# Four window pairs per q and k load, with four rows per partition, in a local attention kernel

## The chip, the cores and the metric

One core of one Trainium2 chip runs the kernel. The metric is device time in microseconds (us), lower is better. Each version was timed beside runs of the kernel before on the same chip. The experiments ran on four chips, on which the kernel before took 977.5 to 978.3 us (medians).

## The reference

Attention inside windows of 64 rows; B=4, S=4096, D=1536, all float32.

```python
q_w = q.reshape(B, nw, W, D)            # W = 64; k_w, v_w likewise
logits = np.einsum('bnwd,bnud->bnwu', q_w, k_w) * D ** -0.5
attn = softmax(logits)                  # over u (cut)
out = np.einsum('bnwu,bnud->bnwd', attn, v_w)
```

The inputs are 302.0 MB and the output 100.7 MB. The arithmetic per byte is small.

## The kernel before

PE is the matmul engine, ACT and DVE the scalar and the vector engine; POOL and SP issue transfers (DMAs). The inputs lie in HBM, tiles in SBUF, and PE writes to PSUM. The kernel works on one pair of windows (128 rows) at a time, 128 pairs in all. q, k and v are cast to bf16 by the DMA itself, issued from POOL. PE transposes q and k in 128x128 blocks, ACT or DVE copies the transposes out of PSUM, PE forms the scores, ACT the exponentials, PE the product with v, and ACT or DVE scales it. SP issues the stores.

```python
q_pool = ctx.enter_context(tc.tile_pool(name="q_pool", bufs=3))   # k_pool, v_pool: 3 too
# ... t_pool, s_pool, o_pool: 2 buffers; PSUM pools: 2, 2 and 3
for it in range(n_pairs):
    r0 = it * P
    nc.gpsimd.dma_start(out=q_nat, in_=qf[r0 : r0 + P, :])   # [128, 1536]; k and v likewise
    for src, dst in ((q_nat, qT), (k_nat, kT)):
        for g in range(DCH // TGRP):                         # 2 groups of 6 blocks
            ptile = ptr_pool.tile([P, TGRP, P], bf16, name="ptile")
            for j in range(TGRP):
                nc.tensor.transpose(ptile[:, j, :], src[:, c * P : (c + 1) * P], ident)
            nc.any.tensor_copy(out=dst[:, g * TGRP : (g + 1) * TGRP, :], in_=ptile)
    # ... scores st (12 matmuls), est = exp(st), row sums, recip
    # ... po = est x v by 64x64 blocks, o_sb = po * recip
    nc.sync.dma_start(out=of[r0 : r0 + P, :], in_=o_sb)
```

The softmax here doesn't subtract the row's maximum and nothing guards it: scores larger than these inputs give would overflow.

## Time and profile before

| | |
|---|---|
| Time, median | 977.8 us (13 runs, 977.3 to 978.8) |
| HBM traffic over the span | 412 GB/s |
| DMA, slices at 9 tenths or more | 39 of 40 |
| PE, ACT, DVE busy | 60%, 42%, 28% |

From the page of the kernel before: the span, busy times, the DMA slices (one digit for each fortieth of the span, in tenths), and the traffic.

```profile
span 976.4 us, 14179 instructions
...
PE 586.0 (60%) x5632; PEld 405.1 (41%) x5632; DVE 273.2 (28%) x513; ACT 412.6 (42%) x641; POOL 203.4 (21%) x390
...
DMA  9999999999999999999999999999999999999996
...
q0 software_dynamic: 55296, 151.02, 78.8%
q1 hardware_dynamic: 18432, 100.67, 26.1%
q8 instruction: 44, 0.72, 0.3%
...
HBM read 301.99 MB, written 100.66 MB: 412 GB/s over the span
```

No compute engine is near full, and DMA has no hole but at the end. The queue lines give packets, MB and the share of 16 engines' time. q0 is the loads (bf16 as landed, half of what is read), q1 the stores. Together they show 105%, as the times of packets overlap. In the DMA records of the trace, a load piece is one partition's row: 6 KB read, 3 KB landed, taking 248 ns of one engine. 49152 of the q0 packets are such pieces and 6144 are 4-byte completion writes, 16 to each of the 384 load DMAs (one per DMA engine).

The page's groups of the kernel before, transposes copied out of PSUM (count, then busy us and mean ns of one):

```profile
L79 ACT COPY qT<-ptile 128x768 bf16<-128x768 bf16 x254 | 202.7, 798 | 250.8 <-PE ptile L76 246.9
...
L79 DVE COPY kT<-ptile 128x768 bf16<-128x768 bf16 x128 | 70.7, 552 | 25.2 <-PE ptile L76 25.1
```

The waits of the kernel before (total us, times, longest):

```profile
PE ptile L76 <- DMA q_nat<-in_q_dram: 220.2, 65, 6.5
...
PE ptile L76 <- DMA k_nat<-in_k_dram: 101.9, 63, 2.6
```

PE waits for data for a third of the time. That is what a DMA-bound kernel looks like from PE.

### The profile page before, as it was taken

To read this page: it belongs to the slowest core of one execution; us is meant where nothing else is said; L and a number is where in the kernel's file an instruction comes from. 1 tells how busy PE (TensorE), PEld (TensorE's weight loads), DVE (VectorE), ACT (ScalarE), POOL (GpSimd) and SP (SyncE) were. 2 spreads that over 40 slices of the span, in tenths; PEclk is the share of its full clock that TensorE was granted. 3 is DMA by queue.
4 is the path that set the end of the run, shared out by engine and by line. 5 is a ranking of instruction groups with operands and counts; after the bars stand their busy time and mean duration, and the time that the engine had idled before them with its cause. 6 is when DMAs were issued, how large, how long until landed. Compare 5 with 4: busy or idle time off the path is not lost.

```text
span 976.4 us, 14179 instructions
## 1 busy us (share of the span) xinstructions
PE 586.0 (60%) x5632; PEld 405.1 (41%) x5632; DVE 273.2 (28%) x513; ACT 412.6 (42%) x641; POOL 203.4 (21%) x390
## 2 busy tenths in 40 slices
PE   5556566565565665656656556556565565565654
PEld 3344344343343443434434344344343443444433
DVE  2223232232232322322323223232232232322322
ACT  3344344443443444434434344344443443444443
POOL 3122121221221212212212222121221221212210
PEclk9676776776767767677777676776776777767676
DMA  9999999999999999999999999999999999999996
GB/s 194 255 268 253 270 261 257 275 254 264 267 253 271 261 256 269 256 267 263 255 274 259 259 270 254 268 263 255 274 259 259 270 251 271 263 255 274 252 265 184
DMA packets 73795, 252.60 MB, mean 259 GB/s; under 512 B 8192, under 2 KB 8192, under 8 KB 73728
## 3 DMA queue, kind: packets, MB, share of 16 engines
q0 software_dynamic: 55296, 151.02, 78.8%
q1 hardware_dynamic: 18432, 100.67, 26.1%
q8 instruction: 44, 0.72, 0.3%
q14 instruction: 23, 0.19, 0.0%
HBM read 301.99 MB, written 100.66 MB: 412 GB/s over the span
## 4 chain that ended last, share of the span: by engine, by line
DMA 82%; PE 9%; issue 7%; ACT 1%; POOL 1%; POOLq 0%; ACTq 0%
DMA k_nat<-in_k_dram 48%; DMA v_nat<-in_v_dram 30%; DMA q_nat<-in_q_dram 4%; PE ptile L76 4%; PE po L108 3%; PE ps L87 1%; POOL k_nat L66 1%; ACT kT L79 0%; PE ps L100 0%; ACT qT L79 0%; ACT o_sb L122 0%; POOL q_nat L65 0%; POOL v_nat L67 0%; ACT est L96 0%; POOLq L66 0%
## 5 line engine op out<-in xcount | busy, mean ns | idle before, releaser
L76 PE MATMUL ptile<-ident,q_nat 128*128 128x128 bf16 x1536 | 181.2, 264 | 220.2 <-DMA q_nat<-in_q_dram 220.2
L79 ACT COPY qT<-ptile 128x768 bf16<-128x768 bf16 x254 | 202.7, 798 | 250.8 <-PE ptile L76 246.9
L76 PE MATMUL ptile<-ident,k_nat 128*128 128x128 bf16 x1536 | 168.4, 264 | 140.5 <-DMA k_nat<-in_k_dram 101.9
L76 PEld LDWEIGHTS <-q_nat 128*128 128x128 bf16 x1536 | 128.4, 121 | 258.4 <-DMA q_nat<-in_q_dram 231.5
L76 PEld LDWEIGHTS <-k_nat 128*128 128x128 bf16 x1536 | 119.9, 118 | 214.6 <-DMA k_nat<-in_k_dram 119.5
L103 DVE RECIPROCAL recip<-ps 128x1 f32<-128x1 f32 x128 | 21.5, 168 | 635.6 <-PE ps L101 618.0
L122 DVE TENSOR_SCALAR o_sb<-po,recip 128x512 f32<-128x512 f32 x254 | 184.9, 748 | 29.9 <-PE po L115 18.4
L87 PE MATMUL ps<-qT,kT 128*128 128x128 bf16 x1536 | 170.6, 267 | 20.8 <-ACT kT L79 19.8
L122 ACT ACTIVATE o_sb<-po,recip 128x512 f32<-128x512 f32 x130 | 89.4, 688 | 147.6 <-PE po L115 146.7
L67 POOL DMA_DIRECT2D v_nat<-in_v_dram x128 | 67.6, 528 | 391.6 <-PE po L115 347.9
L108 PE MATMUL po<-v_nat,est 64*64 64x512 bf16 x384 | 148.5, 509 | 0.0
L115 PE MATMUL po<-v_nat,est 64*64 64x512 bf16 x384 | 148.4, 509 | 0.0
L87 PEld LDWEIGHTS <-kT 128*128 128x128 bf16 x1536 | 128.3, 123 | 40.3 <-ACT kT L79 36.8
L79 ACT COPY kT<-ptile 128x768 bf16<-128x768 bf16 x128 | 102.3, 799 | 56.6 <-PE ptile L76 56.6
L65 POOL DMA_DIRECT2D q_nat<-in_q_dram x128 | 68.3, 533 | 231.3 <-PE ptile L76 206.1
L66 POOL DMA_DIRECT2D k_nat<-in_k_dram x128 | 67.7, 529 | 125.2 <-DMA v_nat<-in_v_dram 84.3
L96 ACT ACTIVATE est<-ps 128x128 bf16<-128x128 f32 x128 | 35.8, 280 | 103.4 <-PE ps L87 103.4
L79 DVE COPY kT<-ptile 128x768 bf16<-128x768 bf16 x128 | 70.7, 552 | 25.2 <-PE ptile L76 25.1
L108 PEld LDWEIGHTS <-est 64*64 64x64 bf16 x384 | 41.1, 138 | 24.4 <-issue 18.8
L115 PEld LDWEIGHTS <-est 64*64 64x64 bf16 x384 | 40.8, 137 | 0.0
L100 PE MATMUL ps<-ones,est 64*64 64x1 bf16 x128 | 25.8, 201 | 3.6 <-ACT est L96 0.4
L100 PEld LDWEIGHTS <-est 64*64 64x64 bf16 x128 | 14.9, 116 | 27.3 <-ACT est L96 13.7
(11 smaller groups left out, 43.7 us busy)
## 6 DMA issues: line engine op xcount, KB each, us to landing
out_dram<-o_sb SPq DMA_DIRECT2D x128, 768.0 KB, 7.8
q_nat<-in_q_dram POOLq DMA_DIRECT2D x128, 384.0 KB, 19.1
k_nat<-in_k_dram POOLq DMA_DIRECT2D x128, 384.0 KB, 19.1
v_nat<-in_v_dram POOLq DMA_DIRECT2D x128, 384.0 KB, 16.6
```

What stands on the lines that cost most here:

```text
L65: nc.gpsimd.dma_start(out=q_nat, in_=qf[r0 : r0 + P, :])
L66: nc.gpsimd.dma_start(out=k_nat, in_=kf[r0 : r0 + P, :])
L67: nc.gpsimd.dma_start(out=v_nat, in_=vf[r0 : r0 + P, :])
L76: nc.tensor.transpose(ptile[:, j, :], src[:, c * P : (c + 1) * P], ident)
L79: nc.any.tensor_copy(out=dst[:, g * TGRP : (g + 1) * TGRP, :], in_=ptile)
L87: nc.tensor.matmul(st, kT[:, c, :], qT[:, c, :], start=(c == 0), stop=(c == DCH - 1),)
L96: nc.scalar.activation(out=est, in_=st, func=mybir.ActivationFunctionType.Exp, scale=scale)
L100: nc.tensor.matmul(rs[0:W, :], est[0:W, 0:W], ones[0:W, :], start=True, stop=True)
L103: nc.vector.reciprocal(out=recip, in_=rs)
L108: nc.tensor.matmul(po[0:W, :], est[0:W, 0:W], v_nat[0:W, c * NCOL : (c + 1) * NCOL], start=True, stop=True,)
L115: nc.tensor.matmul(po[W:P, :], est[W:P, W:P], v_nat[W:P, c * NCOL : (c + 1) * NCOL], start=True, stop=True,)
L122: nc.any.tensor_scalar(out=o_sb[:, c * NCOL : (c + 1) * NCOL], in0=po, scalar1=recip, scalar2=None, op0=mybir.AluOpType.mult,)
```

## The change

The intent: fewer and larger q/k transfers. One load brings four pairs of q, with rows 4p to 4p+3 in partition p, so that the 24 KB of a partition lie together in HBM. The row order is undone when the transposes are copied out of PSUM. v and the output stay as they were, pair by pair. Buffer counts change too, the row sums get a PSUM tile of their own (one buffer), and the first loads are issued ahead of the identity's construction.

```diff
+    RPP = 4 if n_pairs % 4 == 0 else 1
-    q_pool, k_pool, v_pool: bufs=3; s_pool, o_pool: bufs=2          (abridged)
+    qk_pool: bufs=2 (q and k tiles of four pairs), v_pool: bufs=6, s_pool: 3, o_pool: 4
+    def load_qk(it):
+        r0 = it * PAIRS_PER_IT * P
+        qt = qk_pool.tile([P, RPP, D], bf16, name="qt")
+        qsrc = qf[r0 : r0 + RPP * P, :].rearrange("(p r) d -> p r d", p=P, r=RPP)
+        nc.gpsimd.dma_start(out=qt, in_=qsrc)                        # k likewise
 ...
-                for j in range(TGRP):
-                    c = g * TGRP + j
-                    nc.tensor.transpose(ptile[:, j, :], src[:, c * P : (c + 1) * P], ident)
-                nc.any.tensor_copy(out=dst[:, g * TGRP : (g + 1) * TGRP, :], in_=ptile)
+                for j in range(RPP):
+                    nc.tensor.transpose(ptile[:, j, :], src[:, j, c * P : (c + 1) * P], ident)
+                dslice = dst[:, c, :].rearrange("d (p j) -> d p j", j=RPP, p=P)
+                nc.any.tensor_copy(out=dslice, in_=ptile.rearrange("d j p -> d p j"))
+        for m in range(PAIRS_PER_IT):
+            v_nat = prev[m] if it == 0 else load_v(pair)
             (scores, exp, sums, product with v, store: as before, for pair m)
```

More of the change, by code (lines that the diff above doesn't have):

```diff
@@ L31 @@
     assert D % P == 0 and (B * S) % P == 0
+    RPP = 4 if n_pairs % 4 == 0 else 1
+    PAIRS_PER_IT = RPP
+    n_iters = n_pairs // PAIRS_PER_IT
     qf = q.flatten_outer_dims()
@@ L38 @@
     consts = ctx.enter_context(tc.tile_pool(name="consts", bufs=1))
-    ident = consts.tile([P, P], bf16)
-    make_identity(nc, ident)
-    ones = consts.tile([P, 1], bf16)
-    nc.vector.memset(ones, 1.0)
-    q_pool = ctx.enter_context(tc.tile_pool(name="q_pool", bufs=3))
-    k_pool = ctx.enter_context(tc.tile_pool(name="k_pool", bufs=3))
-    v_pool = ctx.enter_context(tc.tile_pool(name="v_pool", bufs=3))
+    qk_pool = ctx.enter_context(tc.tile_pool(name="qk_pool", bufs=2))
+    v_pool = ctx.enter_context(tc.tile_pool(name="v_pool", bufs=6))
     t_pool = ctx.enter_context(tc.tile_pool(name="t_pool", bufs=2))
-    s_pool = ctx.enter_context(tc.tile_pool(name="s_pool", bufs=2))
-    o_pool = ctx.enter_context(tc.tile_pool(name="o_pool", bufs=2))
+    s_pool = ctx.enter_context(tc.tile_pool(name="s_pool", bufs=3))
+    o_pool = ctx.enter_context(tc.tile_pool(name="o_pool", bufs=4))
     ptr_pool = ctx.enter_context(tc.tile_pool(name="ptr_pool", bufs=2, space=bass.MemoryType.PSUM))
     ps_pool = ctx.enter_context(tc.tile_pool(name="ps_pool", bufs=2, space=bass.MemoryType.PSUM))
+    rs_pool = ctx.enter_context(tc.tile_pool(name="rs_pool", bufs=1, space=bass.MemoryType.PSUM))
     po_pool = ctx.enter_context(tc.tile_pool(name="po_pool", bufs=3, space=bass.MemoryType.PSUM))
@@ L56 @@
     assert D % NCOL == 0
-    TGRP = 6 if DCH % 6 == 0 else (4 if DCH % 4 == 0 else (2 if DCH % 2 == 0 else 1))
-    for it in range(n_pairs):
-        r0 = it * P
-        q_nat = q_pool.tile([P, D], bf16, name="q_nat")
-        k_nat = k_pool.tile([P, D], bf16, name="k_nat")
-        v_nat = v_pool.tile([P, D], bf16, name="v_nat")
-        nc.gpsimd.dma_start(out=q_nat, in_=qf[r0 : r0 + P, :])
-        nc.gpsimd.dma_start(out=k_nat, in_=kf[r0 : r0 + P, :])
-        nc.gpsimd.dma_start(out=v_nat, in_=vf[r0 : r0 + P, :])
-        qT = t_pool.tile([P, DCH, P], bf16, name="qT")
-        kT = t_pool.tile([P, DCH, P], bf16, name="kT")
+    def load_qk(it):
+        r0 = it * PAIRS_PER_IT * P
+        qt = qk_pool.tile([P, RPP, D], bf16, name="qt")
+        kt = qk_pool.tile([P, RPP, D], bf16, name="kt")
+        qsrc = qf[r0 : r0 + RPP * P, :].rearrange("(p r) d -> p r d", p=P, r=RPP)
+        ksrc = kf[r0 : r0 + RPP * P, :].rearrange("(p r) d -> p r d", p=P, r=RPP)
+        nc.gpsimd.dma_start(out=qt, in_=qsrc)
+        nc.gpsimd.dma_start(out=kt, in_=ksrc)
+        return qt, kt
@@ new lines, in load_v @@
+    def load_v(pair):
+        r0 = pair * P
+        vt = v_pool.tile([P, D], bf16, name="vt")
+        nc.gpsimd.dma_start(out=vt, in_=vf[r0 : r0 + P, :])
+        return vt
+    preq = load_qk(0)
+    prev = [load_v(p) for p in range(PAIRS_PER_IT)]
+    ident = consts.tile([P, P], bf16)
+    nc.vector.memset(ident, 0.0)
+    make_identity(nc, ident, nomemset=True)
+    ones = consts.tile([P, 1], bf16)
+    nc.vector.memset(ones, 1.0)
+    for it in range(n_iters):
+        q_nat, k_nat = preq if it == 0 else load_qk(it)
+        qT = t_pool.tile([P, DCH, RPP * P], bf16, name="qT")
+        kT = t_pool.tile([P, DCH, RPP * P], bf16, name="kT")
@@ L71 @@
         for src, dst in ((q_nat, qT), (k_nat, kT)):
-            for g in range(DCH // TGRP):
-                ptile = ptr_pool.tile([P, TGRP, P], bf16, name="ptile")
-                for j in range(TGRP):
-                    c = g * TGRP + j
+            for c in range(DCH):
+                ptile = ptr_pool.tile([P, RPP, P], bf16, name="ptile")
+                for j in range(RPP):
                     nc.tensor.transpose(
-                        ptile[:, j, :], src[:, c * P : (c + 1) * P], ident
+                        ptile[:, j, :], src[:, j, c * P : (c + 1) * P], ident
@@ L78 @@
                     )
-                nc.any.tensor_copy(
-                    out=dst[:, g * TGRP : (g + 1) * TGRP, :], in_=ptile
-                )
-        ps = ps_pool.tile([P, P + 8], fp32, name="ps")
-        st = ps[:, 0:P]
-        rs = ps[:, P : P + 1]
-        for c in range(DCH):
-            nc.tensor.matmul(
-                st,
-                kT[:, c, :],
-                qT[:, c, :],
-                start=(c == 0),
-                stop=(c == DCH - 1),
-            )
-        est = s_pool.tile([P, P], bf16, name="est")
@@ L96 @@
-        nc.scalar.activation(
-            out=est, in_=st, func=mybir.ActivationFunctionType.Exp, scale=scale
-        )
-        nc.tensor.matmul(rs[0:W, :], est[0:W, 0:W], ones[0:W, :], start=True, stop=True)
-        nc.tensor.matmul(rs[W:P, :], est[W:P, W:P], ones[W:P, :], start=True, stop=True)
-        recip = s_pool.tile([P, 1], fp32, name="recip")
-        nc.vector.reciprocal(out=recip, in_=rs)
-        o_sb = o_pool.tile([P, D], fp32, name="o_sb")
-        for c in range(D // NCOL):
-            po = po_pool.tile([P, NCOL], fp32, name="po")
-            nc.tensor.matmul(
-                po[0:W, :],
-                est[0:W, 0:W],
-                v_nat[0:W, c * NCOL : (c + 1) * NCOL],
-                start=True,
-                stop=True,
+                if RPP > 1:
+                    dslice = dst[:, c, :].rearrange("d (p j) -> d p j", j=RPP, p=P)
+                else:
+                    dslice = dst[:, c, :].unsqueeze(1)
@@ new lines @@
+                nc.any.tensor_copy(out=dslice, in_=ptile.rearrange("d j p -> d p j"))
+        for m in range(PAIRS_PER_IT):
+            pair = it * PAIRS_PER_IT + m
+            r0 = pair * P
+            v_nat = prev[m] if it == 0 else load_v(pair)
+            st = ps_pool.tile([P, P], fp32, name="st")
+            rs = rs_pool.tile([P, 1], fp32, name="rs")
+            for c in range(DCH):
+                nc.tensor.matmul(
+                    st,
+                    kT[:, c, m * P : (m + 1) * P],
+                    qT[:, c, m * P : (m + 1) * P],
+                    start=(c == 0),
+                    stop=(c == DCH - 1),
+                )
+            est = s_pool.tile([P, P], bf16, name="est")
+            nc.scalar.activation(
+                out=est, in_=st, func=mybir.ActivationFunctionType.Exp, scale=scale
@@ L114 @@
             )
             nc.tensor.matmul(
-                po[W:P, :],
-                est[W:P, W:P],
-                v_nat[W:P, c * NCOL : (c + 1) * NCOL],
-                start=True,
-                stop=True,
-            )
-            nc.any.tensor_scalar(
-                out=o_sb[:, c * NCOL : (c + 1) * NCOL],
-                in0=po,
-                scalar1=recip,
-                scalar2=None,
-                op0=mybir.AluOpType.mult,
-            )
-        nc.sync.dma_start(out=of[r0 : r0 + P, :], in_=o_sb)
+                rs[0:W, :], est[0:W, 0:W], ones[0:W, :], start=True, stop=True
+            )
@@ new lines @@
+            nc.tensor.matmul(
+                rs[W:P, :], est[W:P, W:P], ones[W:P, :], start=True, stop=True
+            )
+            recip = s_pool.tile([P, 1], fp32, name="recip")
+            nc.vector.reciprocal(out=recip, in_=rs)
+            o_sb = o_pool.tile([P, D], fp32, name="o_sb")
+            for c in range(D // NCOL):
+                po = po_pool.tile([P, NCOL], fp32, name="po")
+                nc.tensor.matmul(
+                    po[0:W, :],
+                    est[0:W, 0:W],
+                    v_nat[0:W, c * NCOL : (c + 1) * NCOL],
+                    start=True,
+                    stop=True,
+                )
+                nc.tensor.matmul(
+                    po[W:P, :],
+                    est[W:P, W:P],
+                    v_nat[W:P, c * NCOL : (c + 1) * NCOL],
+                    start=True,
+                    stop=True,
+                )
+                nc.any.tensor_scalar(
+                    out=o_sb[:, c * NCOL : (c + 1) * NCOL],
+                    in0=po,
+                    scalar1=recip,
+                    scalar2=None,
+                    op0=mybir.AluOpType.mult,
+                )
@@ L134 @@
+            nc.sync.dma_start(out=of[r0 : r0 + P, :], in_=o_sb)
 _INS = ['q', 'k', 'v']
```

## The prediction

> **What bounds the kernel now.** The DMA engines. The slices of the page show DMA at 9 tenths or more in 39 of 40 slices; the table of stretches gives a DMA share of 1.07 in every middle stretch of 30.5 us (packet times overlap). PE is busy 60%, ACT 42%, DVE 28%. The chain that ended last is 82% DMA. HBM traffic is 302.0 MB read plus 100.7 MB written: 412 GB/s over the 976.4 us. The Trainium skill, "DMA: Bandwidth & Descriptors", section "Where 436 GB/s comes from", puts the ceiling of the 16 ports at 435 GB/s; 402.65 MB at that rate is 925 us (estimate). So the most that any change of this kind can win is about 4%, and only by making the DMA engines more efficient or by shortening the ends.
>
> **What the change does.** Four pairs share one q load and one k load; each partition then gets 24 KB that lie together in HBM, where now each partition's piece is 6 KB. In the DMA records a 6 KB piece takes 248 ns of an engine, and a 4-byte completion write some 18 ns. Leaving out about 12 us at the two ends where DMA is not full (2.7 us before the first packet, and a tail in which the last pair is computed and stored), 402.65 MB take about 964 us, 39 us above the 925. Spread over 4096 pieces per engine that is 9.4 ns of overhead each (estimate). If the four rows are merged into one piece, q and k go from 2048 pieces per engine to 512 (4096 to 2560 in all): 1536 x 9.4 ns = 14 us saved, all of it on the critical path. Data volume is unchanged.
>
> The evacuations of the transposes go from 512 of 128x768 to 768 of 128x512, reading PSUM with a stride to undo the row interleave. ACT: 799 ns now, about 590 ns then (estimate, from the 768-column copy and the 512-column evictions at 688). DVE: 552 ns now; the skill's "VectorE: DVE Perf Modes", "Mode 2x_1P", asks for unit step, so I expect the copy to lose the fast mode: 600 to 700 ns for 512 columns. ACT plus DVE busy rises from 686 us to about 770, of 1950 available: not critical. PE work is unchanged. An earlier prologue load saves under 1 us.
>
> **What may be lost.** The unit of work is four times larger. Only two q/k buffers and six v buffers exist; PE runs in order, and before, it already waits 220 us for q and 102 us for k with older work queued behind. If the transposes of the next group stand ahead of the scores of this group, v buffers come free late, and POOL, in order, then issues the next q/k late. I expect DMA to stay fed mostly, but this is the main risk. The tail (four pairs to finish after the last q/k) stays about as long.
>
> **Prediction.** 964 us, range 945 to 995. Faster by over 2%: 0.27; within 2%: 0.60; slower by over 2%: 0.13.
>
> **What would show it.** Right: the DMA packets of the software queue fall from 55296 to about 28000 with 12 KB landing pieces, GB/s over the span rises by 1 to 2%, DMA still 9 in all slices, DVE copies slower. Wrong: packets of 3 KB still (no gain, about 978); dips in the DMA slices, or PE waiting for q/k with POOL waiting for po (slower); or a saving per merged piece well above 9 ns (below 945).

## The result, and the profile after

The kernel after takes 970.5 us (median of 8 runs, 969.5 to 970.9). The ratio to the kernel before is 0.992 (95% interval 0.991 to 0.993). Ratios here are the mean time of one kernel's fast runs over that of the other's in the same rounds, so not quite the ratio of the medians. It is 0.8% faster: clear of noise, but under the 2% line.

From the page of the kernel after, the same lines:

```profile
span 969.2 us, 13864 instructions
...
PE 618.9 (64%) x5632; PEld 429.0 (44%) x5632; DVE 336.4 (35%) x578; ACT 449.3 (46%) x833; POOL 102.0 (11%) x197
...
DMA  9999999999999999999999999999999999999994
...
q0 software_dynamic: 27648, 151.01, 75.5%
q1 hardware_dynamic: 18432, 100.67, 26.2%
...
HBM read 301.99 MB, written 100.66 MB: 415 GB/s over the span
```

The packets of the load queue are halved: the four rows did merge. In the DMA records q and k now land in 8192 pieces of 12 KB (24 KB read), 928 ns each. DMA is still full but for the last slice. ACT plus DVE rise from 686 to 786 us.

The copies of the transposes in the kernel after, from the groups, with their waits:

```profile
L98 ACT COPY kT<-ptile 128x512 bf16<-128x512 bf16 x256 | 146.6, 586 | 86.8 <-PE ptile L91 82.7
...
L98 DVE COPY qT<-ptile 128x512 bf16<-128x512 bf16 x129 | 89.2, 691 | 171.3 <-PE ptile L91 171.3
```

DVE takes 691 ns for 512 columns where it took 552 ns for 768. ACT takes 586 ns, in line with its rate before.

I use one number for the steady part below: the **middle rate**, the bytes read or written in HBM by the pieces in the DMA records between 50 and 900 us, over 850 us (a piece that crosses a limit counts with the part inside). Dividing the 402.65 MB by it gives the time at full rate. The end of the last DMA record less that time is what the two **ends** cost.

| | middle rate, GB/s | at full rate, us | last DMA, us | ends, us |
|---|---|---|---|---|
| before | 418.7 | 961.8 | 975.2 | 13.4 |
| after | 422.8 | 952.3 | 967.9 | 15.6 |

So the steady part gained 9.5 us and the ends gave back 2.2. Two questions follow: what the 9.5 us are (I had expected 14), and why the ends grew.

The end shows in the table of stretches. First the kernel before, then after: busy us of PE, PEld (PE's weight loads), DVE, ACT and POOL with counts, PE clock, DMA share, GB/s landed.

```profile
950.00:960.00 10.00, 6.03 (x65) 3.73 (x61) 4.27 (x8) 4.68 (x7) 0.53 (x1) 0.84 1.05 256
960.00:970.00 10.00, 7.16 (x56) 4.86 (x58) 2.40 (x5) 3.54 (x6) 0.00 (x0) 0.50 0.48 157
```

```profile
940.00:950.00 10.00, 8.33 (x63) 5.88 (x61) 4.39 (x7) 5.84 (x12) 0.00 (x0) 0.50 0.84 243
950.00:960.00 10.00, 8.64 (x97) 6.28 (x97) 4.70 (x9) 6.31 (x13) 0.00 (x0) 0.89 0.20 67
960.00:970.00 10.00, 1.74 (x18) 0.62 (x14) 1.70 (x4) 2.70 (x5) 0.00 (x0) 0.79 0.66 270
```

In the kernel after DMA is nearly idle from 950 to 960 us (share 0.20) while PE is busier than in the stretches beside it, and only then come the last stores. The timeline of the kernel after shows how that came about, first POOL, then PE:

```profile
888.56 0.53 POOL L63 DMA_DIRECT2D qt<-in_q_dram  x1 [4.43 <-PE ptile L91]
896.09 0.53 POOL L64 DMA_DIRECT2D kt<-in_k_dram  x1 [7.00 <-DMA qt<-in_q_dram]
898.63 0.53 POOL L70 DMA_DIRECT2D vt<-in_v_dram  x1 [2.01 <-PE rs L125]
```

```profile
937.79 0.63 PE L134 MATMUL po<-vt,est 64*64 64x512 bf16 x1 [7.54 <-DMA vt<-in_v_dram]
...
942.51 1.04 PE L91 MATMUL ptile<-ident,qt 128*128 128x128 bf16 x8
```

PE stood 7.5 us before a product with a v that was not there, and the bulk of the last group's transposes came behind it in program order, from 942 us on. By the semaphore records of the trace, this v is the one issued at 898.63 us: it belongs to the last group but one, but was issued behind the q and k of the last group and landed at 937.7, after them. Over the whole run PE waits 234 us for v in this way. (The chain of waits of the kernel after covers only the last 8 us of the span and is of no use here.)

### The profile page after: what moved, and what is told of

Same layout as the page of the kernel before. It is cut to its first block, busy times and chain, and to the rows that moved or that the text cites. A ratio compares the mean times of both kernels' runs of the same rounds, so it can differ in the third digit from the quotient of the medians.

```text
span 969.2 us, 13864 instructions
## 1 busy us (share of the span) xinstructions
PE 618.9 (64%) x5632; PEld 429.0 (44%) x5632; DVE 336.4 (35%) x578; ACT 449.3 (46%) x833; POOL 102.0 (11%) x197
## 3 DMA queue, kind: packets, MB, share of 16 engines
q0 software_dynamic: 27648, 151.01, 75.5%
q1 hardware_dynamic: 18432, 100.67, 26.2%
## 5 line engine op out<-in xcount | busy, mean ns | idle before, releaser
L134 PE MATMUL po<-vt,est 64*64 64x512 bf16 x384 | 151.8, 503 | 233.8 <-DMA vt<-in_v_dram 233.6
L91 PE MATMUL ptile<-ident,qt 128*128 128x128 bf16 x1536 | 188.6, 278 | 74.6 <-DMA qt<-in_q_dram 39.3
L91 PE MATMUL ptile<-ident,kt 128*128 128x128 bf16 x1536 | 182.5, 259 | 29.0 <-DVE kT L98 11.2
L109 PE MATMUL st<-qT,kT 128*128 128x128 bf16 x1536 | 196.6, 244 | 2.8 <-ACT kT L98 0.2
L91 PEld LDWEIGHTS <-qt 128*128 128x128 bf16 x1536 | 141.9, 128 | 127.5 <-issue 79.7
L98 ACT COPY qT<-ptile 128x512 bf16<-128x512 bf16 x255 | 144.4, 587 | 108.8 <-PE ptile L91 106.9
L98 ACT COPY kT<-ptile 128x512 bf16<-128x512 bf16 x256 | 146.6, 586 | 86.8 <-PE ptile L91 82.7
L91 PEld LDWEIGHTS <-kt 128*128 128x128 bf16 x1536 | 144.3, 119 | 59.9 <-issue 47.5
L141 PE MATMUL po<-vt,est 64*64 64x512 bf16 x384 | 151.8, 503 | 0.0
L98 DVE COPY qT<-ptile 128x512 bf16<-128x512 bf16 x129 | 89.2, 691 | 171.3 <-PE ptile L91 171.3
L98 DVE COPY kT<-ptile 128x512 bf16<-128x512 bf16 x128 | 88.5, 692 | 149.6 <-PE ptile L91 149.6
L129 DVE RECIPROCAL recip<-rs 128x1 f32<-128x1 f32 x128 | 21.1, 165 | 12.7 <-PE rs L125 12.3
```

The source lines that it names most:

```text
L91: nc.tensor.transpose(ptile[:, j, :], src[:, j, c * P : (c + 1) * P], ident)
L98: nc.any.tensor_copy(out=dslice, in_=ptile.rearrange("d j p -> d p j"))
L109: nc.tensor.matmul(st, kT[:, c, m * P : (m + 1) * P], qT[:, c, m * P : (m + 1) * P], start=(c == 0), stop=(c == DCH - 1),)
L129: nc.vector.reciprocal(out=recip, in_=rs)
L134: nc.tensor.matmul(po[0:W, :], est[0:W, 0:W], v_nat[0:W, c * NCOL : (c + 1) * NCOL], start=True, stop=True,)
L141: nc.tensor.matmul(po[W:P, :], est[W:P, W:P], v_nat[W:P, c * NCOL : (c + 1) * NCOL], start=True, stop=True,)
```

## The experiments

Eleven kernels ran besides the two. Theory "pieces": the gain comes from merging the q/k pieces, each piece having a fixed cost. Rivals: fewer DMAs (192 load DMAs in place of 384); buffers and order. For the shortfall: the size of the cost per piece, contention with compute, or the end.

### Small pieces in the kernel after

```diff
-        qt = qk_pool.tile([P, RPP, D], bf16, name="qt")
+        qt = qk_pool.tile([P, RPP, D + 16], bf16, name="qt")[:, :, 0:D]     # kt likewise
```

> The kernel after, with each q/k row padded by 16 elements in SBUF, so that the four rows of a partition can't be merged into one 24 KB piece; same two DMAs per four pairs, same compute, same buffers. Theory 'pieces' (the gain comes from fewer, larger q/k pieces): software-queue packets back to about 52000, rate in the middle falls from 423 to about 418.5 GB/s, time 978 to 981 us (the rate of before plus the longer tail of after). Rival 'fewer DMAs' (gain from 192 instead of 384 load DMAs, with fewer completion writes and POOL issues): stays at 970 to 972. Rival 'buffers and order': also stays at 970 to 972.

Measured: 976.3 us, ratio 0.998, between the two expectations. The load queue shows that the pieces are 3 KB again:

```profile
q0 software_dynamic: 52224, 151.01, 78.6%
```

The middle rate is 419.8, that is 959.2 us at full rate: 6.9 us of the 9.5 are gone. The other 2.6 us stay although the pieces are small. They go with the fewer DMAs (192 completion writes less per engine; 2.6 us / 192 is 14 ns, and a 4-byte record of the load queue takes 18 ns on average in the kernel before), which was not tested apart from the other differences. So "pieces" holds for three quarters; "buffers and order" falls for those.

### The kernel before with the buffers of after

```diff
-    q_pool bufs=3, k_pool bufs=3, v_pool bufs=3, s_pool bufs=2, o_pool bufs=2      (abridged)
+    q_pool bufs=8, k_pool bufs=8, v_pool bufs=6, s_pool bufs=3, o_pool bufs=4
```

> The kernel before, with the buffer counts of after (q and k 8 pairs each, v 6, s 3, o 4). Theory 'pieces': no more than 0.2% faster, 976 to 978 us, as DMA is already full. Rival 'buffers and order': 970 to 972 us.

Measured: 976.2 us, ratio 0.998, middle rate 418.7, the same as before. Deeper buffers do nothing for a queue that is never empty. The 1.6 us are at the ends (11.8 in place of 13.4).

### Two rows per partition

```diff
-    RPP = 4 if n_pairs % 4 == 0 else 1
+    RPP = 2
```

> The kernel after with two rows per partition instead of four: q/k pieces of 12 KB, 1024 instead of 1536 pieces per engine saved against before. Theory 'pieces': middle rate about 421.4 GB/s (two thirds of the gain), so 3 us more than after in the steady part, but a shorter tail by 1 to 3 us: 970 to 974. Rival 'fewer DMAs' gives 972 to 975 (256 load DMAs). If the group size cost is what eats the gain, it is faster than after: 966 to 969.

Measured: 972.9 us, ratio 0.995, middle rate 421.3. Taking from the run with small pieces 4.5 ns for each removed piece (6.9 us / 1536) and 14 ns for each removed completion write, 1024 pieces and 128 writes give 961.8 - 4.6 - 1.8 = 955.4 us at full rate; measured 955.7. The ends cost 13.7 us, 1.9 less than with four rows.

### Twelve v buffers

```diff
-    v_pool = ctx.enter_context(tc.tile_pool(name="v_pool", bufs=6))
+    v_pool = ctx.enter_context(tc.tile_pool(name="v_pool", bufs=12))
```

> The kernel after with 12 instead of 6 v buffers. In after PE waits 234 us in all for v tiles, and at the end it waits 7.5 us for the v of the third pair of the last but one group, which pushes the last group's transposes back, so that DMA runs dry. Theory 'late v makes the tail longer': the wait for v nearly goes, the tail loses 2 to 6 us: 965 to 968. Rival (DMA full in the middle and a tail set by computing four pairs): 969.5 to 971.

Measured: 973.5 us, slower than after; a miss. PE's waits for v do go (it waits 317 us for q instead), but v now comes so far ahead that q and k of the last group are the last loads: in the DMA records they land at 944.5 us (933.4 in after). All the work of four pairs then comes with nothing left to load:

```profile
950.00:960.00 10.00, 8.00 (x95) 5.57 (x92) 3.91 (x8) 6.93 (x14) 0.00 (x0) 1.00 0.09 36
```

DMA share 0.09; the ends cost 17.3 us. The late v was not the whole cause: what matters is how much work hangs on the last loads.

### v issued with its group, eight buffers

```diff
-    v_pool ... bufs=6
+    v_pool ... bufs=8
         q_nat, k_nat = preq if it == 0 else load_qk(it)
+        v_now = prev if it == 0 else [load_v(it * PAIRS_PER_IT + m) for m in range(PAIRS_PER_IT)]
 ...
-            v_nat = prev[m] if it == 0 else load_v(pair)
+            v_nat = v_now[m]
```

> The kernel after with 8 v buffers (one group ahead) and the v loads issued with their group's q and k, so that the last loads to land are the four v of the last group, in order, and v of the group before comes ahead of the last q/k. Six buffers (after) left PE blocked 7.5 us on a late v; twelve moved q/k to the end and lengthened the tail. Theory 'order of the last loads sets the tail': time from the last DMA byte of full rate falls, ends cost 11 to 14 us in place of 15.6, total 966 to 969. Rival 'four pairs of work at the end set the tail whatever the order': 970 to 972.

Measured: 966.4 us, ratio 0.989. The middle rate is that of after (422.8); the ends cost 11.0 in place of 15.6. The last stretches of this run:

```profile
950.00:960.00 10.00, 6.88 (x72) 3.59 (x71) 4.81 (x10) 6.42 (x13) 0.00 (x0) 0.97 0.60 243
960.00:970.00 10.00, 0.00 (x0) 0.00 (x0) 0.00 (x0) 0.00 (x0) 0.00 (x0) 0.66 0.25 102
```

DMA has a share of 0.60 where after had 0.20. v of the last group is the last load (landed by 952.9 us), and the transposes of that group run while it comes in. With six, twelve and eight buffers the middle is equal and the ends are 15.6, 17.3 and 11.0 us.

Against twelve buffers the reading is direct. In both runs the PE instructions of the last groups follow the same pattern, 6.3 us apart (the last product starts at 964.4 and at 958.1 us), and the last q and k land 6.2 us apart (944.5 and 938.3): the order of the loads sets the end. Against six buffers (after) two things differ. No v of the last group but one is behind the last q and k now, so PE isn't held before the last group's transposes. But the granted PE clock also differs between the runs, 0.72 in after and 0.81 here (0.81 with twelve buffers too), and these transposes with the scores among them took 12.3 us in after and 10.8 us here. So up to about 1.5 of the 4.6 us between 15.6 and 11.0 may be the clock; no run separates them.

### A plain last group

The same, with q and k of the last group loaded pair by pair in 6 KB pieces and processed pair by pair.

```diff
+        q_nat, k_nat = preq if it == 0 else (load_qk_plain(it) if last else load_qk(it))
 ...                      # in the last group: for each pair its transposes, then its scores
```

> As the run before, but the last group loads q and k pair by pair in 6 KB pieces and processes pair by pair as the kernel before did; its v stay the last loads. If the tail is set by the grain of the last group, 2 to 5 us less than the run with v by group: 963 to 966. If it is set by the last v and its eviction and store alone: the same as that run within 1 us.

Measured: 970.0 us, slower than the run before it; a miss. The timeline of PE in this run:

```profile
946.67 0.63 PE L156 MATMUL po<-vt,est 64*64 64x512 bf16 x1 [10.14 <-DMA vt<-in_v_dram]
...
948.17 1.89 PE L121 MATMUL ptile<-ident,kt 128*128 128x128 bf16 x12
```

The ends cost 13.5 us. PE stood 10.1 us before the first of the last group's v products. v was issued behind eight small loads of q and k, and most transposes of the other three pairs stand behind that product. A smaller grain at the end is no help when a wait stands in front of it in program order.

### DMA alone, in stages

No compute; wrong output. Each stage is one kind of transfer.

```diff
+    for i in range(n_pairs):  nc.gpsimd.dma_start(out=a, in_=qf[i * P : (i + 1) * P, :])      # A: 6 KB
+    for i in range(n_iters):  nc.gpsimd.dma_start(out=b, in_=... "(p r) d -> p r d" of kf)    # B: 24 KB
+    # C: v as A, beside 64 stores of 6 KB pieces;  D: 32 stores of 6 KB;  E: 8 stores of 24 KB
```

> Wrong result on purpose; DMA alone in stages: q in 6 KB pieces, k in 24 KB pieces, v in 6 KB pieces beside stores of 6 KB pieces, stores of 6 KB pieces, stores of 24 KB pieces. Theory 'overhead per piece is constant': 6 KB loads about 421 GB/s read, 24 KB loads about 431, 6 KB stores about 420, 24 KB stores about 430, and the mixed stage also about 421. Rival 'mixing loads and stores costs more': the mixed stage is slower than both pure ones, about 416, which no merging of q/k pieces would win back.

The table of stretches of this run, stages A, B, C and D (busy us of DVE and POOL, PE clock, DMA share, GB/s landed; in A and B the bytes read are twice those landed):

```profile
20.00:230.00 210.00, 0.00 (x0) 59.61 (x113) 1.00 1.08 212
250.00:465.00 215.00, 0.00 (x0) 17.42 (x33) 1.00 1.02 216
490.00:820.00 330.00, 8.93 (x58) 60.30 (x115) 1.00 1.06 279
840.00:890.00 50.00, 0.00 (x0) 0.00 (x0) 1.00 1.02 415
```

From the DMA records in the same stretches, E from 900 to 950 us; the time of a piece at that rate is 16 engines x its bytes / rate, and 435.2 GB/s is the ceiling that the prediction cites from the skill (225.9 ns for 6 KB, 903.5 ns for 24 KB):

| stage | GB/s in HBM | ns per piece | above the ceiling, ns per piece |
|---|---|---|---|
| A, loads, 6 KB | 423.9 | 231.9 | 6.0 |
| B, loads, 24 KB | 432.3 | 909.6 | 6.1 |
| D, stores, 6 KB | 414.5 | 237.2 | 11.3 |
| E, stores, 24 KB | 429.8 | 914.9 | 11.4 |
| C, 6 KB loads and stores | 419.2 | | |

The cost of a piece, completion writes included (one to eight pieces on each engine), does not depend on its size: 6 ns for a load, 11 ns for a store. The ceiling comes out of the run itself: from 6 to 24 KB a piece takes 677.7 ns more, for loads and for stores, and 18432 B x 16 / 677.7 ns is 435.2 GB/s. The run was made once, but parts of a stage agree within 0.5 GB/s (A: 423.7 to 423.9; D: 414.0 to 414.9). My 9.4 ns was the mean over both kinds. For 1536 load pieces, 6.0 ns gives 9.2 us; the kernels showed 9.5. "Mixing costs" as I had put it (slower than both, about 416) is refused: a mix of A and D in the ratio of C would have 420.7 GB/s, and C had 419.2, between the two. A small cost of mixing, 0.4% here, is not refused. The expected rates of 421 and 420 for A and D were off by 3 and 5.5 GB/s, in opposite directions: the difference between loads and stores that I had missed.

### DMA alone, everything in 24 KB pieces

```diff
+    nc.gpsimd.dma_start(out=vt, in_=fat(vf, it))        # q, k, v; fat: "(p r) d -> p r d", r = 4
+    nc.sync.dma_start(out=fat(of, it), in_=t)
```

> Wrong result on purpose; DMA alone, the same bytes as the kernel, all of q, k, v and the stores in 24 KB pieces. With 4.5 ns per piece and 14 ns per completion write (worked out from the earlier runs) the rate is about 427 GB/s, so 943 us plus about 8 us of ends: 948 to 953. If overhead per piece is nearly all of what is above 925 us: 935 to 940.

Measured: 943.1 us (wrong output), ratio 0.965, middle rate 431.4, 933.3 us at full rate. The stage table gives 925.2 + 768 x 6.1 ns + 256 x 11.4 ns = 932.8 us. The expectation of 948 to 953 rested on 4.5 ns for every piece and was too high. This is roughly the floor of this approach.

### DMA alone, with the transfers of after and of before

```diff
+    # after: q, k by fat loads; v and the stores in 6 KB pieces; each store waits for its group's loads
+    # before: q, k, v and the stores in 6 KB pieces; each store waits for its pair's loads
```

> Wrong result on purpose; DMA alone with the transfers of after: q and k in 24 KB pieces, v and stores in 6 KB pieces, no compute. Theory 'the middle of after is set by DMA pieces alone; slower evacuations, PE waits and store delays cost nothing there': middle rate 422 to 424 GB/s, as in after (422.8). Rival 'part of the expected rate was lost to the compute side (late issues, contention)': 426 GB/s or more, as the prediction's 9.4 ns per piece had it (402.65 MB in 949 us is 424.2; with constant cost).

> Wrong result on purpose; DMA alone with the transfers of the kernel before: everything in 6 KB pieces, 384 loads and 128 stores, no compute. DMA alone with the transfers of after had 424.6 GB/s where after itself had 422.8. Theory 'compute takes a like share of the rate in both kernels, and merging q/k pieces is worth about 6 ns each': about 420.3 GB/s in the middle, 9.5 us more than the DMA of after for the 402.65 MB. Rival 'compute disturbs DMA in after only, and merging is worth the 9.4 ns of the prediction': 418.5 GB/s, the rate of the kernel before, 14 us more than the DMA of after.

Measured: 958.1 us with a middle rate of 424.6 (transfers of after), 970.8 us with 420.2 (transfers of before); both outputs wrong. The first came out above the 422 to 424 I expected, so compute does take some of the rate in after: 948.4 us at full rate alone, 952.3 in the kernel, 3.9 us. But in the kernel before it takes 3.4 us (958.4 and 961.8). Transfers alone gained 10.0 us, the two kernels 9.5. So the larger group and the slower copies cost at most half a us in the middle, and the rival "contention in after" falls.

Two smaller remainders stay open. Transfers alone take longer than the single costs add up to: 925.2 us and the pieces at 6.0 and 11.3 ns make 955.2 us for the transfers of before (measured 958.4) and 946.0 for those of after (948.4); that has the sign and the size of the mixing loss in stage C. And what in compute takes the 3.4 and 3.9 us is in part visible: with compute the DMA engines also carry records of kind "instruction" (the q8 line above, 16 KB and 934 ns each; no q8 in the two runs of transfers alone). Between 50 and 900 us all instruction records fill 2.7 us of each engine in both kernels, and 0.3 and 0.1 us in these runs, if they are spread evenly over the 16 engines (an estimate; no run tests it).

### Large store pieces

If stores are the dear pieces, merge those. The version with v by group, with q in (row mod 4, partition) order, so that four matmuls of 32 columns put row 4p+r of all four pairs into one PSUM tile; the exp tiles keep zeros outside their two windows. The last group stores as before.

```diff
-            for c in range(D // NCOL):                   # per pair: two 64x64 products
+            for r in range(RPP):                         # per group
+                for c in range(D // NCOL):
+                    for m in range(RPP):
+                        nc.tensor.matmul(po[m * Q : (m + 1) * Q, :], est[:, r, :],      # est of pair m
+                            vs[m][:, c * NCOL : (c + 1) * NCOL], start=True, stop=True) # Q = 32
+                    (o_sb[:, r, columns of c] = po * recip[:, r])
+            nc.sync.dma_start(out=fat(of, it), in_=o_sb)
```

> The version with v by group, with the stores in 24 KB pieces too (all groups but the last): each exp tile keeps only its two windows' blocks, and four matmuls of 32 columns put rows 4p+r of all four pairs into one PSUM tile, so that a partition's four output rows lie together. The stage run gave 237.2 ns per 6 KB for small stores and 228.6 for large ones: 992 x 8.6 ns = 8.5 us, plus some 1.3 us for 93 fewer completion writes. Theory 'store pieces are the dear ones': middle rate about 427 GB/s, time 954 to 959 us (the end as in the run with v by group, or a little longer). Rival 'only loads gain': 965 to 967. If PE's or the group barrier's waits reach DMA, slower than 967.

Measured: 956.1 us (5 runs, 955.4 to 958.2), correct, ratio 0.978 to the kernel before. The middle rate is 427.3 as expected, and the ends cost 10.4 us.

```profile
q1 hardware_dynamic: 5040, 100.67, 24.9%
...
HBM read 301.99 MB, written 100.66 MB: 422 GB/s over the span
```

Against the version with v by group, 10.1 us were gained at full rate; 744 store pieces per engine at 11.3 ns are 8.4 us. This includes their 93 completion writes, which the expectation had counted once more, so the hit of 427 is in part luck: 1.7 us stay unexplained in a version that also changes the products and half of the copies. This version beats both kernels. It also shows the copies with and without the stride side by side, as q needs no reordering in it:

```profile
L105 ACT COPY qT<-ptile 128x512 bf16<-128x512 bf16 x276 | 159.3, 590 | 375.7 <-PE ptile L98 372.8
...
L100 DVE COPY kT<-ptile 128x512 bf16<-128x512 bf16 x159 | 110.0, 692 | 133.1 <-PE ptile L98 131.9 <-ACT kT L100 1.2
...
L105 DVE COPY qT<-ptile 128x512 bf16<-128x512 bf16 x96 | 40.2, 419 | 358.5 <-ACT qT L105 335.2 <-PE ptile L98 23.2
```

## Why the prediction was right or wrong

- **The bound: right.** DMA bounds the kernel in every version. The ceiling of 435 GB/s that the Trainium skill states ("DMA: Bandwidth & Descriptors", "Where 436 GB/s comes from") was not passed: the best stage reached 432.3.
- **The mechanism: right.** Rows merged, packets fell from 55296 to 27648, and undoing the merge alone took back 6.9 of the 9.5 us. GB/s over the span rose by 0.7% (412 to 415), less than the 1 to 2% named as the mark; in the middle it rose by 1.0%.
- **The cost of a piece: mis-sized.** The step "that is 9.4 ns of overhead each" gave 14 us; the steady part gained 9.5 us, 6.2 ns per removed piece. I had spread 39 us over all 4096 pieces alike. Load pieces cost 6.0 ns and store pieces 11.3 ns, and 3.4 us belong to compute running beside. The change removes the cheap kind only. 3072 x 6.0 + 1024 x 11.3 ns are 30 us; with the 3.4 us this leaves about 3 us of the 36.6 above the ceiling in the middle of the kernel before (the 3.2 us by which transfers alone exceed the sum; open).
- **The end: mis-sized.** "The tail stays about as long" was 2.2 us short (13.4 to 15.6 us). The mechanism I gave as a risk (program order on PE, v that comes late) is there, but it costs only where no more loads are queued behind. With v issued by group the ends cost 11.0 us.
- **The sum.** 964 was predicted and 970.5 measured, within the range. That says little, as 945 to 995 also holds no change at all; the gain was 7.3 us where 14 were forecast. The piece cost was 4.9 us too kind (14.4 against 9.5) and the end 2.2 us, 7.1 us together for a gap of 6.5; the half us between is within the spread of the runs.
- **The copies: right, and hidden.** ACT 586 ns for an estimated 590; DVE 691 ns in the range of 600 to 700. The skill ("VectorE: DVE Perf Modes", "Mode 2×_1P") asks for unit step; the strided copy took 692 ns and the unit-step copy of the same size 419 ns. ACT plus DVE rose to 786 us (about 770 predicted) and cost nothing that the DMA comparison could show beyond half a us.
- **The main risk did not occur.** PE waits 234 us for v, but DMA stayed full until the end.

## What to carry to other kernels

When the DMA engines are full, count pieces by kind, measure the cost of each kind alone in a kernel of nothing but transfers, and merge the dear kind first; a mean over all kinds mis-sizes the gain. Waits of a compute engine in the middle of this DMA-bound kernel cost next to nothing (PE waited 234 us for v), but the same wait at the end does: what to arrange there is the order of the last loads, so that little work hangs on the last one. More buffers can make that order worse.

## What the Trainium skill lacked or had wrong

- "DMA: Bandwidth & Descriptors", "Why small descriptors are slow (HBM only)": it speaks of a fixed cost per packet with a 256 B example, and of joining descriptors into one packet as worth it only at 256 B or less. Longer descriptors, which is what merging rows makes, this section does not size. Here 6 KB pieces still lost 6.0 ns each as loads and 11.3 ns as stores, and merging to 24 KB gave 2.0% (loads, 423.9 to 432.3 GB/s) and 3.7% (stores, 414.5 to 429.8). That a store piece costs nearly twice a load piece stands on no page.
- The same page, "Anatomy of one DMA — SWDGE (gpsimd) path", calls the semaphore write of a DMA essentially free. In the records a 4-byte completion write takes mostly 9 or 22 ns, 18 ns on average in the load queue of the kernel before. On DMA engines that are full, 192 fewer of them per engine go with a gain of 2.6 us, though not tested apart.
- The same page, "Where 436 GB/s comes from", says that the HBM side (about 358 GB/s) binds transfers between HBM and SBUF; that this needs both cores of the HBM to stream stands only in the note under the measured table. With this core alone, loads ran at 432.3 and the kernels at 412 to 422 GB/s over the whole span.
- "PSUM — Partial Sum Buffer" names a penalty of non-contiguous patterns for matmuls only, and no page says what a step costs ScalarE. Reading PSUM with a step of 128 bf16 elements cost ScalarE nothing (586 ns against 590 ns without); for VectorE it was 692 against 419 ns, in line with "VectorE: DVE Perf Modes".
